# DRAM layout of the chain's operands in a hybrid decoder layer: five loads per half segment in place of ten

## The chip, the cores and the metric

The kernel runs on one core of a Trainium2 chip. The metric is the device time of one execution in microseconds (us), taken as the median of several runs. The engines are named as in the profile: PE (TensorE matmuls), PEld (its weight loads), DVE (VectorE), ACT (ScalarE), POOL (GpSimd), and SP (SyncE), whose queue issues all of the program's DMA transfers.

## The reference, cut to what matters

One layer over 2048 tokens of width 1024: a norm and an input projection, then two groups of eight heads of 64, RWKV-7 time mixing and a forgetting attention (FoX), a SiLU gate over both, the output projection and a final norm. The parts that matter here:

```python
def step(state, inp):                      # RWKV-7, per head: state is 64 x 64, 2048 steps
    rt, wt, kt, vt, kkt, at = inp
    sa = jnp.einsum('bhvk,bhk->bhv', state, -kkt)
    state = (state * wt[:, :, None, :] + sa[..., :, None] * (kkt * at)[..., None, :]
             + vt[..., :, None] * kt[..., None, :])
    yt = jnp.einsum('bhvk,bhk->bhv', state, rt)
    return state, yt
...
c = jnp.cumsum(log_f, axis=1)              # FoX: decay of each head along the sequence
s = jnp.einsum('bhqd,bhkd->bhqk', q, k) * scale + c[..., :, None] - c[:, :, None, :]
prob = softmax(where(causal, s, -inf)); o = prob @ v
```

## The kernel before, in words

The 2048 steps of RWKV-7 are cut into 32 chunks of 64 tokens. Heads go in pairs `p` (0 to 3); a pair fills the 128 partitions, head `h` of the pair in partitions 0 to 63 or 64 to 127 (`HR`).

First comes a preparation stage: for each pair and each block of 512 tokens, `prep` makes the operands of the chunks and stores them to DRAM. For half a block (four chunks) these are `d_ga` (lines 526 to 530), `d_gl` (line 550), `d_ar` (line 551), `d_nk` (line 562), and for a whole block `d_vn` (line 572). `inverse` adds `d_z`. FoX projections and gate projections are put between these pieces.

Then comes the chain: `chain` (line 724) runs the 32 chunks in order, because each needs the state of the one before. Its operands come back in half segments of two chunks: `half_seg` (line 703) loads a tile `G` from `d_ga` and `d_gl`, a tile `SV` from `d_vn`, `NK` and `AR`. `G` holds, for each pair and head, 64 partitions that come from `d_ga` and the other 64 that come from `d_gl`; `SV` holds values in one half of the partitions and the running state, which the chain writes itself, in the other. Each of the four tiles has three buffers, and a half segment is asked for four chunks ahead.

The attention of the FoX heads fills PE around the chain. `decay_setup` (line 873) prepares the decay of two heads and stores its two fp16 halves to `d_nc` (line 918); `head_max` (line 930) loads queries and keys of a head, and two rows of `d_nc` into `km` (line 939), and multiplies them (`sq`, line 952) to find row maxima; `head_loads` and `head_out` do the attention proper (`st`, `pv`).

The order of the instructions on each engine is not that of the text: the program is built with a planner that simulates a timeline (`schedule_with_timeline_sim=True`) and fixes each engine's queue by it. On the chip each queue then runs strictly in that order, SP's DMA queue included.

Of the kernel before, what the change touches and what calls it, by code (L numbers as in the profile page):

```python
# [20 lines left out]
S = 2048  # L21
# [18 lines left out]
def hymba_body(tc, x, norm_g, w_in, rw_mu, rw_w_up, rw_w0, rw_a_up, rw_a0, rw_k_k, rw_k_a, rw_r_k,  # L40
# [7 lines left out]
    with ctx:  # L48
# [3 lines left out]
        def dram(name, shape, dt=F32):  # L52
            return dr.tile(shape, dt, name=name)

        d_ga = dram("d_ga", [512, 32, 128])
        d_gl = dram("d_gl", [4, 128, 32, 128])
        d_ar = dram("d_ar", [4, 128, 32, 64])
        d_nk = dram("d_nk", [4, 128, 32, 128])
        d_vn = dram("d_vn", [4, 128, 32, 64])
        d_z = dram("d_z", [4, 128, 32, 64])  # L60
        d_bo = dram("d_bo", [512, S])
        d_q = [dram(f"d_q{i}", [512, S], F16) for i in range(2)]
# [2 lines left out]
        d_l = dram("d_l", [NB, 128, 2, TB])  # L65
        d_yr = dram("d_yr", [512, S])
        d_gate = dram("d_gate", [1024, S])
        d_nc = [dram(f"d_nc{i}", [8, S], F16) for i in range(2)]
        d_gs = dram("d_gs", [4, S], F16)
        d_yf = dram("d_yf", [S, 512])  # L70

# [339 lines left out]
        with c1:  # L411
# [59 lines left out]
            def prep(p, b, r, k, v, lw, mab):  # L471
# [48 lines left out]
                for hb in range(2):  # L520
                    h4 = slice(4 * hb, 4 * hb + 4)
                    hs = slice(8 * b + 4 * hb, 8 * b + 4 * hb + 4)
                    v_ = f"{u}_{hb}"
                    bk = T("bk" + v_, "bk", 2, (128, 4, 128))

                    ga = T("ga" + v_, "ga", 2, (128, 4, 128))
                    nc.vector.scalar_tensor_tensor(ga[:, :, 0:64], c3(nk)[:, h4], -1.0, c3(nlw)[:, h4],
                                                   ALU.mult, ALU.mult)
                    nc.gpsimd.tensor_tensor(ga[:, :, 64:128], c3(r)[:, h4], c3(nL)[:, h4], ALU.mult)
                    nc.sync.dma_start(d_ga[pc, hs, :], ga)  # L530

                    nc.vector.scalar_tensor_tensor(bk[:, :, 0:64], c3(th)[:, h4], 0.5, c3(eI)[:, h4], ALU.mult, ALU.mult)
                    nc.gpsimd.tensor_tensor(bk[:, :, 64:128], c3(k)[:, h4], c3(eI)[:, h4], ALU.mult)

                    gl = T("gl" + v_, "o2", 2, (128, 4, 128))
                    ar = T("ar" + v_, "ar", 1, (128, 4, 64))
                    pb = ps_r.tile([128, 4, 128], F32, name=f"pb{v_}", tag="r")
                    pk = ps_r.tile([128, 4, 128], F32, name=f"pk{v_}", tag="r")
                    for c in range(4):
                        for h, (q0, q1) in enumerate(HR):  # L540
                            nc.tensor.matmul(pb[q0:q1, c], bk[q0:q1, c, 0:64], ga[q0:q1, c], start=True, stop=True)
                        for h, (q0, q1) in enumerate(HR):
                            o0, o1 = HR[1 - h]
                            nc.tensor.matmul(pk[o0:o1, c], bk[q0:q1, c, 64:128], ga[q0:q1, c], start=True, stop=True)
                    nc.vector.tensor_tensor(mab[:, :, hs].rearrange("q t c -> q c t"), pb[:, :, 0:64],
                                            mk[:, 0:64].unsqueeze(1).to_broadcast([128, 4, 64]), ALU.mult)
                    nc.vector.tensor_tensor(ar, pb[:, :, 64:128],
                                            mk[:, 64:128].unsqueeze(1).to_broadcast([128, 4, 64]), ALU.mult)
                    nc.vector.tensor_tensor(gl, pk, mk.unsqueeze(1).to_broadcast([128, 4, 128]), ALU.mult)
                    nc.sync.dma_start(d_gl[p, :, hs, :], gl)  # L550
                    nc.sync.dma_start(d_ar[p, :, hs, :], ar)

                    nc.gpsimd.tensor_tensor(bk, bk, gam[:, p, hs].unsqueeze(2).to_broadcast([128, 4, 128]), ALU.mult)
                    nkt = T("nkt" + v_, "o2", 2, (128, 4, 128))
                    pn = ps_r.tile([128, 4, 128], F32, name=f"pn{v_}", tag="r")
                    for c in range(4):
                        nc.tensor.transpose(pn[:, c, :], bk[:, c, :], ident)
                    nc.scalar.activation(nkt[:, :, 0:64], pn[:, :, 0:64], AF.Copy)
                    for h, (q0, q1) in enumerate(HR):
                        o0, o1 = HR[1 - h]  # L560
                        nc.scalar.activation(nkt[o0:o1, :, 64:128], pn[q0:q1, :, 64:128], AF.Copy)
                    nc.sync.dma_start(d_nk[p, :, hs, :], nkt)
# [5 lines left out]
                for h in range(2):  # L568
                    o0, o1 = HR[1 - h]
                    for par, (q0, q1) in enumerate(HR):  # L570
                        nc.scalar.activation(vn[o0:o1, :, par, :], pv[q0:q1, :, h * 64:h * 64 + 64], AF.Copy)
                nc.sync.dma_start(d_vn[p, :, c8, :], vn.rearrange("q c e d -> q (c e) d"))

            def inverse(p, mab):

# [127 lines left out]
        def half_seg(hs):  # L703

            c2_ = slice(2 * hs, 2 * hs + 2)
            g_ = rp.tile([128, 4, 2, 2, 128], F32, name=f"G{hs}", tag="G", bufs=3)
            nk_ = rp.tile([128, 4, 2, 2, 64], F32, name=f"NK{hs}", tag="NK", bufs=3)
            ar_ = rp.tile([128, 4, 2, 64], F32, name=f"AR{hs}", tag="AR", bufs=3)
            sv_ = rp.tile([128, 2, 4, 2, 64], F32, name=f"SV{hs}", tag="SV", bufs=3)
            ga_v = d_ga.rearrange("(p q) c x -> q p c x", q=128)  # L710
            gl_v = d_gl.rearrange("p q c x -> q p c x")
            vn_v = d_vn.rearrange("p q c x -> q c p x")
            for h, (q0, q1) in enumerate(HR):
                o0, o1 = HR[1 - h]
                nc.sync.dma_start(g_[q0:q1, :, h], ga_v[q0:q1, :, c2_])
                nc.sync.dma_start(g_[o0:o1, :, h], gl_v[o0:o1, :, c2_])
                for c in range(2):
                    nc.sync.dma_start(sv_[o0:o1, c, :, h, :], vn_v[o0:o1, 2 * hs + c])
            nc.sync.dma_start(nk_.rearrange("q p c h d -> q p c (h d)"),
                              d_nk.rearrange("p q c x -> q p c x")[:, :, c2_])  # L720
            nc.sync.dma_start(ar_, d_ar.rearrange("p q c x -> q p c x")[:, :, c2_])
            return g_, nk_, ar_, sv_
# [107 lines left out]
        with c2:  # L830
# [42 lines left out]
            def decay_setup(p):  # L873
# [37 lines left out]
                nc.tensor.transpose(p3, f(w_), ident)  # L911
                nct = A(f"nct{p}", "nct", (32, 128))
                ts(nct, p3, -1.0 / GS, ALU.mult)
                nch = [A(f"nch{p}_{i}", f"nch{i}", (32, 128), F16) for i in range(2)]
                nc.vector.tensor_copy(nch[0], nct)
                nc.vector.tensor_tensor(nch[1], nct, nch[0], ALU.subtract)
                for i in range(2):
                    nc.sync.dma_start(d_nc[i][hs].rearrange("h (j q) -> (h j) q", q=128), nch[i])

            def v_setup(h):  # L920

# [8 lines left out]
            def head_max(h):  # L930
# [4 lines left out]
                nc.sync.dma_start(qb[0:64], d_q[0][r])  # L935
                nc.sync.dma_start(qb[64:66], d_gs[2:4])
                nc.sync.dma_start(km[0:64], d_k[0][r])
                for i in range(2):
                    nc.sync.dma_start(km[64 + i:65 + i], d_nc[i][h:h + 1])
                mx = ap_.tile([128, 16, 4], F32, name=f"mx{h}", tag="mx", bufs=2)  # L940
                nc.gpsimd.memset(mx, -3e38)
                for i in range(16):
# [213 lines left out]
```

## Time and profile before

| | |
|---|---|
| median of 3 runs | 1705.23 us (1697.16 to 1711.42) |
| the profiled execution | 1702.15 us, of which its span is 1700.4 us |
| PE, DVE, ACT, POOL busy | 92%, 67%, 52%, 45% of the span |
| mean granted TensorE clock | 0.963 |
| bytes moved | 207.71 MB, 122 GB/s in the mean |
| packets under 512 B, under 2 KB | 53664, 173472 of 211979 |

All parts below are read from the one profiled execution; the span runs from its first to its last instruction. A busy PE is a PE with a matmul in its pipeline, at whichever clock was granted. The idle time of an engine that does not set the end costs nothing.

### The profile page before, as it was taken

What the parts mean: (1) busy time and instruction counts of PE and PEld (TensorE: products, weight loads), DVE (VectorE), ACT (ScalarE), POOL (GpSimd) and SP (SyncE); (2) the same over time, 40 slices, a digit from 0 to 9 for tenths busy, and PEclk for the clock granted to TensorE, in tenths of its full rate; (3) what the DMA queues carried; (4) which work ended last, traced back from release to release, by engine and by line L of the source; (5) the groups of instructions that cost most, each with busy time, mean ns of one, the idle gap of its engine ahead of it and who ended that gap; (6) DMA issues with size and microseconds to landing.
All of it is one profiled execution on the core that took longest, in us unless ns stands there. A gap on an engine that the chain in (4) does not pass through costs nothing. (4 is left out here: it accounts for less than half of the span.)

```text
span 1700.4 us, 36186 instructions
## 1 busy us (share of the span) xinstructions
PE 1571.5 (92%) x14182; PEld 970.9 (57%) x14182; DVE 1137.3 (67%) x2442; ACT 889.1 (52%) x1683; POOL 756.8 (45%) x846
## 2 busy tenths in 40 slices
PE   4899799899999999899999999799999998899998
PEld 2455355455554564445454566566666665577886
DVE  5876468975797758843654578488898674754443
ACT  5634444444424454445334238487787868776221
POOL 5654554555335543532201126366666755753000
PEclk9799899999999999999999999799999998999999
DMA  6432232233213242322326019858688632733452
GB/s 181 124 100 87 96 109 90 83 121 116 98 68 119 78 149 85 118 84 85 117 84 157 32 45 226 194 137 199 158 198 193 163 85 67 227 100 101 156 172 87
DMA packets 211979, 207.71 MB, mean 122 GB/s; under 512 B 53664, under 2 KB 173472, under 8 KB 211296
## 3 DMA queue, kind: packets, MB, share of 16 engines
q1 hardware_dynamic: 211808, 205.39, 42.1%
q8 instruction: 112, 1.84, 0.5%
q14 instruction: 59, 0.48, 0.1%
HBM read 123.34 MB, written 81.94 MB: 121 GB/s over the span
## 5 line engine op out<-in xcount | busy, mean ns | idle before, releaser
L1010 POOL TENSOR_TENSOR pl<-p,ph 128x512 f16<-128x512 f32 (+3 forms) x216 | 233.2, 1088 | 172.7 <-ACT p L1008 135.2
L1007 ACT ACTIVATE ph<-st,be 128x512 f16<-128x512 f32 (+1 forms) x320 | 202.4, 633 | 95.0 <-PE st L1003 40.3
L956 DVE TENSOR_REDUCE mx<-sq 128x1 f32<-128x384 f32 (+6 forms) x320 | 184.7, 603 | 50.8 <-PE sq L955 31.4
L1008 ACT ACTIVATE p<-st,be 128x512 f32<-128x512 f32 (+1 forms) x320 | 202.7, 634 | 5.5 <-POOL pl L1010 3.4
L332 PE MATMUL pf<-fh_f,hhi 128*128 128x386 f16 x512 | 169.5, 332 | 2.1 <-DVE fl L348 2.1
L332 PE MATMUL pf<-fl_f,hhi 128*128 128x386 f16 x512 | 168.2, 328 | 1.2 <-POOL fl_f L219 1.2
L332 PE MATMUL pf<-fh_f,hlo 128*128 128x386 f16 x512 | 168.5, 329 | 0.0
L254 PE MATMUL pj_r<-hhi,wh_r 128*128 128x512 f16 x384 | 148.9, 388 | 0.0
L254 PE MATMUL pj_r<-hlo,wh_r 128*128 128x512 f16 x384 | 148.7, 387 | 0.0
L254 PE MATMUL pj_r<-hhi,wl_r 128*128 128x512 f16 x384 | 148.5, 387 | 0.0
L341 POOL TENSOR_TENSOR fr<-ft,nhalf 128x4 f32<-128x4 f32 x64 | 65.3, 1021 | 175.1 <-DVE ft L101 169.0
L332 PEld LDWEIGHTS <-hhi 128*128 128x128 f16 x1024 | 99.3, 99 | 75.6 <-issue 12.0
L1018 PE MATMUL pv<-va,pl 128*128 128x65 f16 x1088 | 131.4, 196 | 7.7 <-POOL pl L1010 4.3
L1014 PE MATMUL pv<-va,ph 128*128 128x65 f16 x1088 | 131.8, 196 | 2.6 <-DVE ot L1023 1.7
L1016 PE MATMUL pv<-vb,ph 128*128 128x64 f16 x1088 | 131.7, 194 | 0.0
L952 PE MATMUL sq<-km,qb 66*128 66x384 f16 (+6 forms) x320 | 107.9, 357 | 21.6 <-DMA km<-d_nc 14.7
L254 PEld LDWEIGHTS <-wh_r 128*128 128x128 f16 x768 | 75.6, 100 | 87.3 <-issue 9.2
L1018 PEld LDWEIGHTS <-pl 128*128 128x128 f16 x1088 | 101.5, 98 | 32.8 <-POOL pl L1010 11.5
L999 PE MATMUL st<-qa,ka 128*128 128x512 f16 (+1 forms) x320 | 113.9, 358 | 5.4 <-ACT p L1008 3.5
L1000 PE MATMUL st<-qb,kb 68*128 68x512 f16 (+1 forms) x320 | 113.8, 358 | 0.8 <-DMA kb<-d_gs 0.8
L1014 PEld LDWEIGHTS <-ph 128*128 128x128 f16 x1088 | 102.0, 99 | 17.6 <-DVE ot L1023 2.6
L1010 DVE TENSOR_TENSOR pl<-p,ph 128x512 f16<-128x512 f32 (+3 forms) x104 | 77.2, 742 | 44.4 <-ACT p L1008 31.5
(376 smaller groups left out, 4005.2 us busy)
## 6 DMA issues: line engine op xcount, KB each, us to landing
d_ga<-ga SPq DMA_DIRECT2D x32, 256.0 KB
d_gl<-gl SPq DMA_DIRECT2D x32, 256.0 KB
d_nk<-nkt SPq DMA_DIRECT2D x32, 256.0 KB
d_gate<-gv SPq DMA_DIRECT2D x32, 256.0 KB
G<-d_ga SPq DMA_DIRECT2D x32, 256.0 KB
G<-d_gl SPq DMA_DIRECT2D x32, 256.0 KB
NK<-d_nk SPq DMA_DIRECT2D x16, 512.0 KB
xr<-in_x_dram SPq DMA_DIRECT2D x16, 512.0 KB
```

The costliest lines, as they stand in the source:

```text
L254: nc.tensor.matmul(ps, a[:, kt, o:o + 128], h[:, kt, :], start=n == 0, stop=n == 3 * KT - 1)
L332: nc.tensor.matmul(ps, a[:, kt, js], w[:, kt, :], start=n == 0, stop=n == 3 * KT - 1)
L952: nc.tensor.matmul(ps[:, :w], qb[0:66, i * 128:i * 128 + 128], km[0:66, ks], start=True, stop=not last)
L956: nc.vector.tensor_reduce(mx[:, i, b:b + 1], ps[:, :w], AX.X, ALU.max)
L999: nc.tensor.matmul(ps[:, c0:], ka[:, k0:k0 + 128], qa[:, q0 + c0:q0 + 512], start=True, stop=False)
L1000: nc.tensor.matmul(ps[:, c0:], kb[0:68, k0:k0 + 128], qb[0:68, q0 + c0:q0 + 512], start=False, stop=not diag)
L1007: nc.scalar.activation(ph[:, c0:], ps[:, c0:], AF.Exp, bias=be[:, h, qb_, j:j + 1])
L1008: nc.scalar.activation(p32[:, c0:], ps[:, c0:], AF.Exp, bias=be[:, h, qb_, j:j + 1])
L1010: eng.tensor_tensor(pl[:, c0:], p32[:, c0:], ph[:, c0:], ALU.subtract)
L1014: nc.tensor.matmul(pv[:, qq, 0:65], ph[:, s_], vh[:, j, 0:65], start=j == 0 and qq == 0, stop=False, skip_group_check=True)
L1016: nc.tensor.matmul(pv[:, qq, 0:64], ph[:, s_], vl[:, j], start=False, stop=False, skip_group_check=True)
L1018: nc.tensor.matmul(pv[:, qq, 0:65], pl[:, s_], vh[:, j, 0:65], start=False, stop=fin, skip_group_check=True)
```

## The change

`d_ga` and `d_gl` become one tensor `d_g`, laid out by pair and head, in the order in which the tile `G` holds its 128 partitions; `prep` stores each of the two operands in two halves of 64 partitions. One load of 128 partitions (1 MB) then fills `G` where there were four of 64 partitions (256 KB each). `d_vn` is laid out by partition and chunk, so that two loads fill `SV` where there were four; its store now writes runs of 256 B (64 values of one chunk and pair) in place of 2 KB. The two halves of the decay become one tensor `d_nc`, stored one head at a time, and one load of two partitions brings both rows of a head to `km` where there were two. All values, matmuls and bytes moved stay as they are.

```diff
-        d_ga = dram("d_ga", [512, 32, 128])
-        d_gl = dram("d_gl", [4, 128, 32, 128])
+        d_g = dram("d_g", [4, 2, 128, 32, 128])
-        d_vn = dram("d_vn", [4, 128, 32, 64])
+        d_vn = dram("d_vn", [128, 32, 4, 64])
-        d_nc = [dram(f"d_nc{i}", [8, S], F16) for i in range(2)]
+        d_nc = dram("d_nc", [8, 2, S], F16)
...                                                       in prep
-                    nc.sync.dma_start(d_ga[pc, hs, :], ga)
+                    for h, (q0, q1) in enumerate(HR):
+                        nc.sync.dma_start(d_g[p, h, q0:q1, hs, :], ga[q0:q1])
-                    nc.sync.dma_start(d_gl[p, :, hs, :], gl)
+                    for h, (q0, q1) in enumerate(HR):
+                        o0, o1 = HR[1 - h]
+                        nc.sync.dma_start(d_g[p, h, o0:o1, hs, :], gl[o0:o1])
-                nc.sync.dma_start(d_vn[p, :, c8, :], vn.rearrange("q c e d -> q (c e) d"))
+                nc.sync.dma_start(d_vn[:, c8, p, :], vn.rearrange("q c e d -> q (c e) d"))
...                                                       in half_seg
-            for h, (q0, q1) in enumerate(HR):
+            nc.sync.dma_start(g_.rearrange("q p h c x -> q (p h) (c x)"),
+                              d_g.rearrange("p h q c x -> q (p h) c x")[:, :, c2_].rearrange("q a c x -> q a (c x)"))
+            for h in range(2):
                 o0, o1 = HR[1 - h]
-                nc.sync.dma_start(g_[q0:q1, :, h], ga_v[q0:q1, :, c2_])
-                nc.sync.dma_start(g_[o0:o1, :, h], gl_v[o0:o1, :, c2_])
-                for c in range(2):
-                    nc.sync.dma_start(sv_[o0:o1, c, :, h, :], vn_v[o0:o1, 2 * hs + c])
+                nc.sync.dma_start(sv_[o0:o1, :, :, h, :].rearrange("q c p d -> q (c p) d"),
+                                  d_vn[o0:o1, c2_].rearrange("q c p d -> q (c p) d"))
...                                                       in decay_setup
-                for i in range(2):
-                    nc.sync.dma_start(d_nc[i][hs].rearrange("h (j q) -> (h j) q", q=128), nch[i])
+                nch = A(f"nch{p}", "nch", (32, 2, 128), F16)
+                nc.vector.tensor_copy(nch[:, 0], nct)
+                nc.vector.tensor_tensor(nch[:, 1], nct, nch[:, 0], ALU.subtract)
+                for h in range(2):
+                    nc.sync.dma_start(d_nc[2 * p + h].rearrange("i (j q) -> j i q", q=128), nch[16 * h:16 * h + 16])
...                                                       in head_max
-                for i in range(2):
-                    nc.sync.dma_start(km[64 + i:65 + i], d_nc[i][h:h + 1])
+                nc.sync.dma_start(km[64:66], d_nc[h])
```

## Rows read from the trace of the kernel before

**Rows 1.** The page, part 1, its line of engines.
```profile
PE 1571.5 (92%) x14182; PEld 970.9 (57%) x14182; DVE 1137.3 (67%) x2442; ACT 889.1 (52%) x1683; POOL 756.8 (45%) x846
```

**Rows 2.** Stretches: start:end, length, busy us and count by engine, PE clock, DMA share, GB/s.
```profile
core 0: us, PE busy (x) PEld busy (x) DVE busy (x) ACT busy (x) POOL busy (x), PEclk, DMA share, GB/s
1036.00:1071.30 35.30, 34.05 (x577) 23.65 (x576) 27.86 (x64) 27.13 (x53) 20.15 (x21) 1.00 1.06 244
1071.30:1080.90 9.60, 0.06 (x2) 0.13 (x2) 0.00 (x0) 0.00 (x0) 1.11 (x3) 0.62 0.73 132
1080.90:1097.40 16.50, 16.50 (x143) 10.77 (x143) 7.50 (x18) 6.75 (x14) 4.60 (x6) 0.50 0.83 187
1097.40:1418.00 320.60, 307.46 (x4915) 213.18 (x4915) 257.46 (x540) 251.82 (x481) 202.74 (x207) 0.99 0.67 157
```

**Rows 3.** Waits of PE over the whole span: total, times, longest (us).
```profile
PE sq L952 <- DMA km<-d_nc: 14.7, 3, 9.5
...
PE sq L952 <- DMA qb<-d_q: 2.9, 2, 1.6
```

**Rows 4.** The chain that ended last, 1060 to 1083 us: start, length, what.
```profile
1062.28 0.52 SPq L715
...
1065.01 9.94 DMA G<-d_gl
1075.01 4.01 DMA d_nc<-nch
...
1079.36 1.47 DMA km<-d_nc
```

**Rows 5.** Timeline of SP's queue, 1062.8 to 1081.3 us: start, length, issue.
```profile
1065.01 0.66 SPq L716 DMA_DIRECT2D G<-d_gl  x1
...
1069.51 0.53 SPq L719 DMA_DIRECT2D NK<-d_nk  x1
1070.33 3.56 SPq L718 DMA_DIRECT2D SV<-d_vn  x3
1075.01 1.25 SPq L918 DMA_DIRECT2D d_nc<-nch  x2
```

**Rows 6.** Timeline of SP's queue, 1111 to 1120 us.
```profile
1111.57 0.36 SPq L1025 DMA_DIRECT2D d_yf<-ot  x1
1112.07 0.59 SPq L715 DMA_DIRECT2D G<-d_ga  x1
...
1114.01 0.61 SPq L716 DMA_DIRECT2D G<-d_gl  x1
1119.24 0.36 SPq L719 DMA_DIRECT2D NK<-d_nk  x1
```

**Rows 7.** Three stretches in which one kind of transfer filled the DMA queue.
```profile
1112.00:1113.50 1.50, 1.50 (x21) 0.89 (x20) 1.50 (x5) 0.97 (x3) 0.00 (x0) 1.00 0.45 90
1115.00:1118.00 3.00, 3.00 (x59) 2.20 (x56) 3.00 (x6) 2.95 (x7) 3.00 (x3) 1.00 1.13 206
1121.00:1122.00 1.00, 1.00 (x24) 0.76 (x21) 0.97 (x2) 0.88 (x3) 0.85 (x3) 1.00 1.04 358
```

**Rows 8.** Timeline of SP's queue, 1199 to 1204 us.
```profile
1199.69 0.92 SPq L918 DMA_DIRECT2D d_nc<-nch  x2
1202.32 1.53 SPq L939 DMA_DIRECT2D km<-d_nc  x4
```

**Rows 9.** Two stretches around an idle PE, and one after a short wait.
```profile
718.85:722.20 3.35, 0.00 (x1) 0.02 (x1) 3.35 (x7) 0.54 (x1) 2.08 (x4) 0.97 0.55 205
722.20:728.80 6.60, 6.59 (x40) 3.16 (x41) 4.32 (x9) 0.88 (x3) 2.81 (x5) 0.50 0.17 62
1204.60:1210.00 5.40, 5.40 (x91) 3.96 (x92) 5.11 (x10) 4.07 (x7) 2.31 (x2) 1.00 0.25 63
```

**Rows 10.** Waits of SP's queue over the span, and the issues that write d_ga.
```profile
SPq L530 <- DVE ga L527: 72.5, 25, 7.3
...
L530 SPq DMA_DIRECT2D d_ga<-ga x32: 319/320/383, 94.3 to 793.5; - x32
```

More of the change, by code (lines that the diff above doesn't have):

```diff
@@ L709, in half_seg @@
             sv_ = rp.tile([128, 2, 4, 2, 64], F32, name=f"SV{hs}", tag="SV", bufs=3)
-            ga_v = d_ga.rearrange("(p q) c x -> q p c x", q=128)
-            gl_v = d_gl.rearrange("p q c x -> q p c x")
-            vn_v = d_vn.rearrange("p q c x -> q c p x")
-            for h, (q0, q1) in enumerate(HR):
+            nc.sync.dma_start(g_.rearrange("q p h c x -> q (p h) (c x)"),
+                              d_g.rearrange("p h q c x -> q (p h) c x")[:, :, c2_].rearrange("q a c x -> q a (c x)"))
+            for h in range(2):
                 o0, o1 = HR[1 - h]
-                nc.sync.dma_start(g_[q0:q1, :, h], ga_v[q0:q1, :, c2_])
-                nc.sync.dma_start(g_[o0:o1, :, h], gl_v[o0:o1, :, c2_])
-                for c in range(2):
-                    nc.sync.dma_start(sv_[o0:o1, c, :, h, :], vn_v[o0:o1, 2 * hs + c])
+                nc.sync.dma_start(sv_[o0:o1, :, :, h, :].rearrange("q c p d -> q (c p) d"),
+                                  d_vn[o0:o1, c2_].rearrange("q c p d -> q (c p) d"))
             nc.sync.dma_start(nk_.rearrange("q p c h d -> q p c (h d)"),
@@ L913, in decay_setup @@
                 ts(nct, p3, -1.0 / GS, ALU.mult)
-                nch = [A(f"nch{p}_{i}", f"nch{i}", (32, 128), F16) for i in range(2)]
-                nc.vector.tensor_copy(nch[0], nct)
-                nc.vector.tensor_tensor(nch[1], nct, nch[0], ALU.subtract)
-                for i in range(2):
-                    nc.sync.dma_start(d_nc[i][hs].rearrange("h (j q) -> (h j) q", q=128), nch[i])
+                nch = A(f"nch{p}", "nch", (32, 2, 128), F16)
[3 more added lines that the diff above has]
+                    nc.sync.dma_start(d_nc[2 * p + h].rearrange("i (j q) -> j i q", q=128), nch[16 * h:16 * h + 16])
             def v_setup(h):
```

## The prediction, made before the change was run

> **What bounds the kernel now.** I read the page first, then the stretches, then PE's waits, and last the chain that ended last. PE is busy for 1571.5 of 1700.4 us [rows 1], far above any other engine: matmuls set the time, and an edit on transfers can give back only what PE loses by waiting and by a lowered clock. The idle time is about 129 us, and transfers of this change's kind stand behind one large piece of it. In the chain's stage PE does 0.06 us of work between 1071.3 and 1080.9 us, and the stretch after it, 16.5 us long, runs at a granted clock of 0.50 (the 1.2 GHz level) where the stretches beside it have 0.99 to 1.00 [rows 2]. The waits name the cause: `sq` waits for `km<-d_nc`, 14.7 us in three waits, the longest 9.5 [rows 3]. Nothing in PE's waits names `G`, `SV`, `NK` or `AR`: the chain's own loads come in time.
>
> The chain of waits tells why `km` was late [rows 4]. The decay had been computed and the issue of its store to `d_nc` came at 1075.01, after 9.94 us in which SP's queue hung on the landing of a `G` load issued at 1065.01; the store took 4.01 us to be seen, the load of `km` 1.47. The store has nothing to do with that `G` load. Between the two, SP's timeline shows seven issues: `km<-d_k`, two to `qb`, `NK`, three to `SV` [rows 5]. So the store is the eighth transfer after it, and I read this as a queue that lets about eight transfers be under way: each issue first waits for the landing of the eighth before it. The three `SV` issues, 3.56 us for three where one alone takes about 0.6, are held in the same way [rows 5]. This is the place where fewer and larger transfers can count.
>
> The cost of this stall now: 9.5 us of idle time, and 16.5 us at half clock, in which PE does what it could do in 8.25. Together 17.8 us.
>
> **The change part by part. The load of G.** Four issues of 256 KB become one of 1 MB. Where `G` loads alone fill the queue (issues at 1112.07 to 1114.01, 64 partitions each [rows 6]) the rate is 206 GB/s at a full DMA share; where an `NK` load of 128 partitions is alone (issue at 1119.24, held a while by its buffer [rows 6]) it is 358 GB/s [rows 7]. Both move runs of 1 KB, so what differs is the partitions. I therefore let the new load run at 358: 1.05 MB take 2.9 us for 5.1, 2.2 us less in each of 16 half segments, 35 us of transfer time in all. Nearly all of that is hidden beside the chain. What counts is the load just ahead of the `d_nc` store, and it enters below as a shorter time for that store; the bound on the other side is 206 GB/s as now, with the store as slow as now.
>
> Two pages of the Trainium skill differ here. "DMA: Bandwidth & Descriptors", Rules for kernel authors, says that transfers to two partition halves serialize because each half already uses all 16 engines, by which the rate of a half would be that of the whole. "SBUF — State Buffer", Door 1: The DMA port swizzle, says that bandwidth follows the number of ports that the partitions reach, half of them for 64 partitions. The trace's 206 against 358 sides with the second; by the first alone the store would stay at its 4.0 us below and the stall would be 1.4 us longer.
>
> **Issues in the chain's stage.** Each half segment loses five issues of some 0.6 us, 16 times 3 us; SP is no bound there, so this is hidden beside the chain. What counts is the place in the count of eight: the store of `d_nc` then has `G`, `km<-d_k`, two to `qb`, `NK` and one or two `SV` ahead of it, six or fewer, and its eighth predecessor is older than the `G` load. So it isn't held by landings. It still stands behind `NK`, which went out at 1069.51 [rows 5], waiting for the chain to free its buffer, and behind two `SV` issues: 1069.5 + 0.6 + 2 x 0.6 = 1071.3 us, 3.7 earlier than now. From the issue of this store to that of the load that reads it, the quieter case of another pair of heads takes 1202.32 - 1199.69 = 2.6 us [rows 8], against 4.0 here; I take 2.6, as the faster `G` has drained by then, and keep 4.0 for the range. Then 1.5 us for the load and 0.3 for its issue: `sq` starts at 1075.7 in place of 1080.9. The idle time falls from 9.5 to 4.4 us.
>
> **The clock.** After an idle stretch of 3.35 us in the preparation the clock was 0.50 for 6.6 us; after the wait of about 2.3 us that ended at 1204.6 it stayed at 1.00 [rows 9]. With 4.4 us the first is nearer: 6.6 us at half clock, 3.3 us lost, against 8.25 now. The stall costs 4.4 + 3.3 = 7.7 us in place of 17.8: **10.1 us gained**. The bounds are 0 (the order or the queue keeps it as it is) and 17.8 (the planner puts the store ahead of `NK`, where it could go out at 1065.01 + 0.66, about 1066, and land in time).
>
> **The load of km.** One load for two rows of a head. The other two waits of `sq` on it sum to 14.7 - 9.5 = 5.2 us [rows 3]. They go through the same store and one issue less: four `km` issues take 1.53 us [rows 8], two would take half. I count 0.4 us each, **0.8 us**; the bounds are 0 and 5.2, and 2.9 more for the waits on `qb<-d_q` [rows 3], which stand in the same queue.
>
> **The stores.** Each of 32 `d_ga` and 32 `d_gl` stores becomes two: 64 issues more of 0.32 us, 20.5 us of SP over the preparation [rows 10]. SP waits 72.5 us for `ga` at these very issues [rows 10]: it arrives early, so this is covered, and I count 0. Behind it stand the weight loads and `lw`; if the cover were gone the price would be 0.64 us in each of 32 half blocks, 20.5 us at most. The 16 `d_vn` stores now write runs of 256 B. The nearest row is the `d_yf` store of 128 KB in such runs (issue at 1111.57 [rows 6]), at 90 GB/s with a DMA share of 0.45 [rows 7]: 0.26 MB then take 2.9 us each. `SV` is read only in the chain's stage, when the preparation has ended, so nobody waits: 0. Even if all were paid, 16 x 2.9 = 46 us of transfers lie in a stage in which PE does not name `d_vn`. The same DMA page, Specifications, states that runs under 512 B lose line rate to read-modify-write; it bears on these stores alone.
>
> **The order.** The planner lays every queue anew when the transfers change. The trace of before can't show the result; its nearest price is one more or one fewer stall such as the one above, 17.8 us either way. I take 0.
>
> **The sum.** 1702.15 - 10.1 - 0.8 = 1691.3 us against the profiled execution, which lies 3.1 us below the median of the runs. Against the median: 1705.2 - 10.9 = **1694 us**, 0.6% faster. The three runs of before spread by 14 us, so a change of about 1% is what a measurement of this kernel can tell from none.
>
> **The rivals.** *The stall goes wholly.* The store is placed early enough, the clock stays up, and the small waits shrink too: 1705.2 - 17.8 - 5 = 1682 us. For it: the chain names a landing as what releases the store, not the engine that makes the decay [rows 4], so the decay was ready by 1065, and the planner sees fewer issues on SP. Against: in SP's order `NK` and its buffer wait come first, and PE's order puts `sq` where the planner believes the data to be. *Nothing moves.* The bytes are the same, and `sq` needs a store and a load that run one after the other through the same queue; if the planner moves `sq` forward by what SP gains, the wait is as long: 1705 us. For it: the DMA share is 1.06 from 1036 to 1071 [rows 2], full whatever the count of transfers. *A longer queue in front of the small transfers, slower.* Eight places now hold at most 512 KB each (`NK`); with loads of 1 MB they hold more bytes, and a small store or `km` row issued behind them waits for all of them. It decides when SP's order puts a 1 MB load between `d_nc` and `km` of a later pair, where now the waits are 2 us: then one more stall of the same size, 1705.2 + 17.8 = 1723 us. Against: in a queue served in order the bytes ahead of a given transfer are the same.
>
> **How the numbers follow.** The forecast has 0.42 (1688 to 1703), the stall gone 0.23, nothing 0.20, slower 0.15. The range leaves out the slower case and the far end of the stall gone: 1677 to 1714, the upper end being "nothing" plus half of the spread of the runs, with rounding. Faster by over 1% means under 1688: the second case and about a fourth of the first, 0.34; slower by over 1% is 0.15; the rest is 0.51.
>
> **What would show it.** In the changed kernel's profile: `G` loads at some 350 GB/s where they are alone; the `d_nc` store issued within 2 us of `NK` and not released by a `G` landing; PE's wait for `km<-d_nc` at 4 to 5 us, with a short stretch at 0.50 behind it; no wait of PE on `G` or `SV`; the preparation as long as before. The prediction is wrong if a wait of 9 us or more stands in the chain's stage again, under whatever name, or if the preparation's length moves by more than some 10 us, which would be the planner's order and not the transfers.

## The result, and the profile after

The changed kernel takes 1687.65 us (median of six runs) where the kernel before takes 1706.95 beside it: a ratio of 0.9891, with a 95% interval of 0.9859 to 0.9923. It is about 1.1% faster. One of the six runs, 1780.67 us at a mean granted clock of 0.844, was a slow one, and the ratio leaves it out. The profiled execution takes 1691.52 us, of which its span is 1689.8.

The page's line of engines answers to [rows 1]. PE's busy time is 2.4 us less, the span 10.6 us: the same matmuls, with less idle time and a higher clock (0.969 in the mean, 0.963 before).

```profile
PE 1569.1 (93%) x14182; PEld 968.4 (57%) x14182; DVE 1135.4 (67%) x2442; ACT 890.4 (53%) x1683; POOL 756.3 (45%) x846
```

To find where the 10.6 us lie, I cut both spans at the same instructions: the last `pj_r` (the preparation of the chain ends), the last `pf` (the FoX projections end), the last `pY` (the chain ends). The stretches of before, columns as in [rows 2]:

```profile
773.20:1020.40 247.20, 240.80 (x1793) 130.14 (x1792) 140.29 (x365) 93.77 (x166) 49.08 (x57) 0.99 0.27 86
1020.40:1418.00 397.60, 372.03 (x5817) 256.65 (x5816) 308.24 (x655) 299.95 (x575) 238.69 (x246) 0.96 0.72 168
1418.00:1700.40 282.40, 261.82 (x1984) 198.17 (x1982) 137.66 (x210) 141.69 (x286) 95.30 (x86) 0.97 0.42 134
```

and of the changed kernel:

```profile
772.50:1024.90 252.40, 243.95 (x1793) 131.18 (x1792) 139.78 (x365) 94.07 (x167) 49.31 (x57) 0.98 0.28 85
1024.90:1404.20 379.30, 366.28 (x5814) 253.66 (x5813) 308.07 (x655) 299.72 (x575) 238.88 (x246) 0.99 0.68 176
1404.20:1689.80 285.60, 262.60 (x1985) 198.22 (x1984) 136.05 (x210) 142.35 (x286) 94.01 (x86) 0.96 0.41 133
```

The chain's stretch falls from 397.6 to 379.3 us, 18.3 less, and its clock rises from 0.96 to 0.99. The stretch ahead of it grows by 5.2 us and the one behind by 3.2; the preparation ends at 772.5 in place of 773.2. PE's waits, which answer to [rows 3]:

```profile
PE sq L950 <- DMA km<-d_nc: 4.6, 2, 4.2
...
PE sq L950 <- DMA qb<-d_gs: 1.7, 2, 1.3
```

and SP's own waits from 1055 to 1078 us:

```profile
SPq L937 <- DMA d_nc<-nch: 3.8, 1, 3.8
...
SPq L917 <- DMA G<-d_g: 0.7, 1, 0.7
```

Of the 4.6 us for `km`, 4.2 are the wait for the first pair of heads, ahead of the chain's stage. At the second pair, where 9.5 us were lost, 0.4 is left. The stretch up to the first `sq` there, the one behind it (at a clock of 1.00, where [rows 2] had 0.50), and the new `G` load alone:

```profile
1068.90:1076.00 7.10, 5.90 (x125) 4.65 (x122) 4.57 (x11) 4.93 (x12) 4.17 (x5) 1.00 0.66 112
1076.00:1092.00 16.00, 15.80 (x240) 11.13 (x240) 11.30 (x27) 11.04 (x22) 8.44 (x11) 1.00 1.01 275
1104.00:1105.00 1.00, 1.00 (x18) 0.68 (x17) 1.00 (x3) 1.00 (x3) 1.00 (x2) 1.00 1.04 359
```

The new load runs at 359 GB/s, against 206 for the four of before [rows 7]. SP's timeline at this place answers to [rows 5]:

```profile
1058.65 1.33 SPq L712 DMA_DIRECT2D G<-d_g  x1
1060.08 3.44 SPq L936 DMA_DIRECT2D km<-d_k  x1
1063.60 0.58 SPq L978 DMA_DIRECT2D qb<-gh  x1
1064.28 0.54 SPq L979 DMA_DIRECT2D qb<-gl  x1
1064.91 0.54 SPq L718 DMA_DIRECT2D NK<-d_nk  x1
1065.56 2.32 SPq L716 DMA_DIRECT2D SV<-d_vn  x2
1067.92 0.62 SPq L720 DMA_DIRECT2D AR<-d_ar  x1
1069.33 1.37 SPq L917 DMA_DIRECT2D d_nc<-nch  x2
1074.53 0.57 SPq L937 DMA_DIRECT2D km<-d_nc  x2
```

The `d_nc` store is the eighth transfer behind the `G` load, as it was before: there is one `SV` issue less between them, but `AR` moved ahead. And SP's wait names the landing of that `G` load as what let the store go. So the store is held by the same rule; it only goes out earlier.

Where the eight comes from stands in the two traces: each transfer of SP tells its landing by a semaphore, and there are eight of them, used in strict turn (810 of the 818 transfers of before have the semaphore of the eighth before them). The store shares one with the `G` load and goes out 0.06 us after its last update, at 1075.01 after 1074.95 us before and at 1069.33 after 1069.27 here. The count is thus that of the program's semaphores. How many transfers the queue itself would hold is shown by no run.

How much earlier the store goes out has to be counted from PE's place in the program, because PE came here later than before (the stretch ahead grew). The matmul `cumT`, PE's last step in the decay's computation for this pair, is such a mark; it starts at 1060.3 us in the trace of before and at 1064.8 here. PE was free for `sq` 11.0 us after it before, where it began to wait at 1071.3 [rows 2], and 10.8 here (1076.0 less the wait of 0.4). The last instruction that makes the decay's halves ends 3.3 us after the mark in both. The store went out 14.7 us after the mark before, and 4.5 here: that is where the stall went. Which part of the 10.2 us is the `G` load's own, and which was there before, is counted below, beside the run that brings the stall back.

### The profile page after: what moved, and what is told of

Same layout as the page of the kernel before. It is cut to its first block, busy times and chain, and to the rows that moved or that the text cites. A ratio compares the mean times of both kernels' runs of the same rounds, so it can differ in the third digit from the quotient of the medians.

```text
span 1689.8 us, 36160 instructions
## 1 busy us (share of the span) xinstructions
PE 1569.1 (93%) x14182; PEld 968.4 (57%) x14182; DVE 1135.4 (67%) x2442; ACT 890.4 (53%) x1683; POOL 756.3 (45%) x846
## 5 line engine op out<-in xcount | busy, mean ns | idle before, releaser
L1016 PEld LDWEIGHTS <-pl 128*128 128x128 f16 x1088 | 101.3, 98 | 36.8 <-DVE pl L1008 10.4
L950 PE MATMUL sq<-km,qb 66*128 66x384 f16 (+6 forms) x320 | 106.8, 354 | 10.3 <-DMA km<-d_nc 4.6
```

Of the source, the lines that this page charges most:

```text
L1016: nc.tensor.matmul(pv[:, qq, 0:65], pl[:, s_], vh[:, j, 0:65], start=False, stop=fin, skip_group_check=True)
```

## The experiments

The theory to be tested is the width: what shortens the stall is the rate of the `G` loads, by their 128 partitions, since SP's issues wait for landings. A load of 128 partitions is called wide here, one of 64 narrow. The rivals are the count (fewer transfers in the queue of eight) and the order (the planner laid the queues anew). The first four were run on one chip beside the kernel before, the next four and the last four likewise; ratios are to the kernel before that was run beside them.

**G alone.** The new layout and single load of `G`, with the rest as before.

```diff
...                                                       layout and stores of d_g as in the change
+            nc.sync.dma_start(g_.rearrange("q p h c x -> q (p h) (c x)"), d_g...[:, :, c2_]...)
             for h in range(2):
-                nc.sync.dma_start(g_[q0:q1, :, h], ga_v[q0:q1, :, c2_])
-                nc.sync.dma_start(g_[o0:o1, :, h], gl_v[o0:o1, :, c2_])
```

> The kernel before with the G part of the change alone: d_g laid out by head, stores in halves, one load of 128 partitions and 1 MB; SV and d_nc as before. Queue theory (the d_nc store was held by the landings of the eighth transfer before it, and fewer transfers ahead free it): three issues fewer ahead of the store, it goes out some 5 us earlier after the cumulative sum than before (14.6 us there), PE's longest wait for km falls from 9.5 to 0 to 3 us, time 1688 to 1694. Rate theory (64-partition loads run at 206 GB/s, 128-partition loads at 350): the same sign, 1690 to 1697. Rival, order (the planner's new queue order is what helped, not the transfers): the stall may stay or not, time anywhere within 10 us of 1706.

Measured: 1696.61 us, 0.9965 (0.9939 to 0.999). The stall at the second pair shrinks to 1.6 us, but the third and fourth pairs now wait 3.5 and 4.3:

```profile
PE sq L952 <- DMA km<-d_nc: 12.9, 4, 4.3
```

**G by four wide loads.** The same layout, one load of 128 partitions for each pair: the old number of transfers at the new width.

```diff
+            for p in range(4):
+                nc.sync.dma_start(g_[:, p]..., d_g[p]...[:, :, c2_]...)
```

> As the G part alone, but G is loaded by four transfers of 256 KB, one for each pair, of 128 partitions each: as many issues as before, wider. This parts the two theories. Rate theory: G loads at some 350 GB/s, the landings ahead of the d_nc store come 2 us sooner for each half segment in the queue, the wait for km falls to 3 to 6 us, time 1692 to 1699. Queue theory alone: as many transfers as before, the store is held as before, wait 8 to 10 us, time 1702 to 1710.

Measured: 1705.2 us, 1.0016 (0.9996 to 1.0037). The stall at the second pair is 2.1 us, so four wide loads shorten it nearly as one does; but the time is that of before, and at the fourth pair a wait of 7.9 us appears. SP's timeline there shows how: the two stores of the decay's halves are parted by four held `SV` issues, 4.50 us for four.

```profile
1292.88 0.32 SPq L919 DMA_DIRECT2D d_nc<-nch  x1
1293.30 0.38 SPq L720 DMA_DIRECT2D NK<-d_nk  x1
1293.86 4.50 SPq L719 DMA_DIRECT2D SV<-d_vn  x4
1299.79 0.38 SPq L722 DMA_DIRECT2D AR<-d_ar  x1
1300.27 0.45 SPq L919 DMA_DIRECT2D d_nc<-nch  x1
...
1301.65 0.24 SPq L940 DMA_DIRECT2D km<-d_nc  x1
```

So the time is the one expected of the count, but the stall is not: it falls even below what was expected of the rate, and the other waits take the gain away.

**G by two narrow loads.** The new layout, loaded in two halves of 64 partitions: fewer transfers at the old width.

```diff
+            for q0, q1 in HR:
+                nc.sync.dma_start(g_[q0:q1]..., d_g...[q0:q1, :, c2_]...)
```

> As the G part alone, but G is loaded by two transfers of 512 KB, each of 64 partitions: half the issues of before, the old width. Rate theory alone: 206 GB/s as before, the wait for km stays at 8 to 10 us, time 1702 to 1710. Queue theory: two issues fewer ahead of the store, it is held by a transfer two places earlier, the wait falls to 3 to 7 us, time 1692 to 1700.

Measured: 1713.03 us, 1.0057 (1.0036 to 1.0079); 8.7 us at the second pair. Two narrow loads in place of four gain nothing; the kernel is 0.6% slower.

**SV alone.** The layout of `d_vn` and the two `SV` loads.

```diff
-        d_vn = dram("d_vn", [4, 128, 32, 64])
+        d_vn = dram("d_vn", [128, 32, 4, 64])
...                                                       store of d_vn as in the change
-                for c in range(2):
-                    nc.sync.dma_start(sv_[o0:o1, c, :, h, :], vn_v[o0:o1, 2 * hs + c])
+                nc.sync.dma_start(sv_[o0:o1, :, :, h, :]..., d_vn[o0:o1, c2_]...)
```

> The kernel before with the SV part of the change alone: d_vn by partition and chunk, its store in runs of 256 B, two loads for four; G as before. Queue theory: two issues of 1.3 us that were held by landings go from in front of the d_nc store, which goes out 2 to 3 us sooner; wait for km 6 to 8 us, time 1699 to 1706. Rate theory: no change, the SV loads stay at 64 partitions. If the 256 B runs of the store cost anything it is in the preparation: its end (last pj_r matmul at 773 us before) moves by more than 3 us; expected 0.

Measured: 1705.66 us, 1.0013 (0.9991 to 1.0035). The preparation ends no later (last `pj_r` at 769.0 us; 768.0 with the decay rows alone, which leave it as it is), so the stores in runs of 256 B cost nothing there. The waits on `km` move to the later pairs, 19.4 us in four. At the second pair the wait is 3.8 us, but not because the store is early: it goes out 12.4 us after `cumT`, and PE, in another order, is free for `sq` only 16.2 us after it, where it was 11.0 before.

**The decay rows alone.** One tensor `d_nc`, stored per head, one load for both rows.

```diff
...                                                       layout and stores of d_nc as in the change
-                for i in range(2):
-                    nc.sync.dma_start(km[64 + i:65 + i], d_nc[i][h:h + 1])
+                nc.sync.dma_start(km[64:66], d_nc[h])
```

> The kernel before with the d_nc part of the change alone: one store and one load of km for a head where there were two halves each; G and SV as before. Of the runs so far, the G part alone gave 0.9965, the SV part 1.0013, so the sum of the parts misses the whole (0.989) by some 10 us. Theory 1, the round trip d_nc to km is what PE waits for and this part shortens it for all pairs: waits for km from 14.7 us to under 8, time 1692 to 1698. Theory 2, the part does nothing by itself (0.3 us an issue), the whole is more than its parts because it needs a short queue ahead of the store as well: time 1702 to 1710 with the wait of 8 to 10 us where it was.

Measured: 1715.09 us, 1.0053 (1.003 to 1.0076), with 11.0 us at the second pair. The order of PE's instructions here is that of "G by two narrow loads" in all but 14 of 14182 places, and the ratio is the same: four narrow loads or two, under one order. That speaks against the count, though the two differ in the decay rows as well. The time lies above both ranges that were expected.

**The change without the decay rows.** `G` and `SV` as changed, `d_nc` as before.

```diff
...                                                       layout and stores of d_nc as before
-                nc.sync.dma_start(km[64:66], d_nc[h])
+                for i in range(2):
+                    nc.sync.dma_start(km[64 + i:65 + i], d_nc[i][h:h + 1])
```

> The change without its d_nc part. If the queue ahead of the store (G and SV) is what counts: 1686 to 1693, as the whole change, the waits for km under 5 us. If the d_nc part or the order that the planner makes with it is needed: 1697 to 1705, with waits of 3 to 5 us at the later pairs as in the run with the G part alone.

Measured: 1695.12 us, 0.9948 (0.9926 to 0.9971). No wait on `km` at the second and third pairs, 3.3 us at the fourth. The decay rows, which alone make the kernel slower, are worth some 0.5% as the last part of the whole (0.9948 here, 0.9891 and 0.9911 with them). That fourth wait goes with them; but PE's order changes in 4871 places too, so what the rest comes from is not shown.

**The decay early, in both kernels.** The decays of pairs 0 to 2 are computed at once ahead of the attention, so that their stores lie well before their loads.

```diff
-                        if h % 2 == 0:
-                            decay_setup((h + 2) // 2)
+                        if h == -2:
+                            for p in range(3):
+                                decay_setup(p)
+                        elif h == 4:
+                            decay_setup(3)
```

> The kernel before with its layouts and transfers as they are; the decays of pairs 0 to 2 are prepared one after the other ahead of the attention, pair 3 as before. This takes the round trip d_nc to km out of the chain's stage for pairs 1 and 2 without touching a chain load. If the waits for km are what the chain's loads cost PE: no wait of 9 us in the chain's stage, 17.8 us for the stall and some 2 for the second wait gone, time 1682 to 1690. Rival, the waits only show a limit that lies elsewhere (the chain's own latency, the DMA bytes): another wait takes their place and the time is 1698 to 1708.

> The changed kernel with the same early decays. If nothing but the round trip to km was gained by the change, it has little left to win here and ends within 5 us of the early decays with the old transfers, both at 1680 to 1688. If wider and fewer loads are worth something of their own (shorter stretches of a full DMA queue, qb and ka loads sooner), it is 5 to 12 us faster than those: 1672 to 1682.

Measured: 1727.72 us in the kernel before, 1.0147 (1.0116 to 1.0177), and 1721.33 in the changed one, 1.0099 (1.007 to 1.0127). No wait of PE names `km` any more; others, of up to 5.7 us, stand in its place, here in the kernel before:

```profile
PE sq L952 <- DMA qb<-d_q: 6.3, 2, 4.6
PE pU L749 <- DMA zc<-d_z: 5.7, 1, 5.7
PE sq L952 <- DMA qa<-d_q: 4.5, 1, 4.5
```

Both are slower than any of the ranges expected. Taking the wait away in this way is thus no gain. Why the whole becomes 1.5% slower than before is not settled: the planner laid every queue anew. The change is still worth 6.4 us between these two, without any wait on `km`.

**The changed kernel again, and its G by two narrow loads.** The first is the changed kernel, unedited, to measure the other against. The second loads `G` in two halves and leaves all else as changed.

```diff
-            nc.sync.dma_start(g_.rearrange("q p h c x -> q (p h) (c x)"), d_g...)
+            for q0, q1 in HR:
+                nc.sync.dma_start(g_[q0:q1]..., d_g...[q0:q1, :, c2_]...)
```

> The changed kernel once more, unchanged, beside the three below on one chip: ratio to the kernel before 0.986 to 0.993 (1684 to 1694 us), PE's waits for km in the chain's stage under 2 us. It tells how much of the distance between the whole and its parts is noise.

> The changed kernel with G loaded by two transfers of 64 partitions (512 KB each) in place of one of 128; layouts, stores, SV and d_nc as in the change. One issue more for each half segment, and the old width. If the width of the load is what pays: G loads back at 206 GB/s, 2.2 us later for each half segment, and the wait for km returns at the second pair with 5 to 9 us; 1698 to 1710 us. If the number of transfers is what pays: within 4 us of the changed kernel.

Measured: 1687.9 us, 0.9911 (0.9884 to 0.9937), and 1706.66 us, 1.0035 (1.0011 to 1.0059). The two run the same order on DVE, ACT and POOL, and on PE in all but 18 of 14182 places; SP's queue has the second `G` issue and takes some other issues ahead of this place in another order, though from this `G` load to the store the order is the same. So under one order of the compute engines the width of `G`, with what SP's queue makes of it, is worth 18.8 us, no less than the whole gain beside it (16.2). In the repeat, the chain's stretch:

```profile
1021.00:1396.00 375.00, 361.76 (x5813) 250.78 (x5812) 307.88 (x655) 299.20 (x575) 238.90 (x246) 1.00 0.69 178
```

and PE's only wait for `km` in it, at the second pair:

```profile
PE sq L950 <- DMA km<-d_nc: 1.0, 1, 1.0
```

With the narrow loads the stall is back. The stretch in which PE does nothing, the one behind it at half clock, and a stretch in which `G` alone is loaded:

```profile
1074.50:1081.00 6.50, 0.00 (x0) 0.00 (x0) 0.00 (x0) 0.00 (x0) 1.10 (x3) 0.76 0.56 96
1081.00:1108.50 27.50, 27.43 (x235) 17.65 (x235) 12.27 (x27) 11.64 (x23) 8.12 (x9) 0.50 0.81 184
1121.00:1123.00 2.00, 2.00 (x38) 1.44 (x35) 2.00 (x5) 1.95 (x5) 2.00 (x2) 1.00 1.15 208
```

It costs 6.5 us of idle time, and 27.5 us at 0.50 in which 13.7 are lost: 20.3 us. It is the stall of [rows 2], 3.1 us shorter in idle time and 11 longer at the low clock. This execution takes 1717.27 us, 10.6 above its kernel's median, so the 27.5 us need not be usual; what the stall costs in the median run is not shown. SP's queue there:

```profile
1062.45 2.81 SPq L713 DMA_DIRECT2D G<-d_g  x2
...
1068.20 0.53 SPq L720 DMA_DIRECT2D NK<-d_nk  x1
...
1074.44 2.72 SPq L919 DMA_DIRECT2D d_nc<-nch  x2
1079.45 0.58 SPq L939 DMA_DIRECT2D km<-d_nc  x2
```

and SP's wait ahead of the store:

```profile
SPq L919 <- DMA G<-d_g: 1.5, 1, 1.5
```

The store again goes out when a `G` load has landed, the eighth transfer before it. Counted from `cumT`, with the issues of `G` from each SP timeline:

| us after `cumT` | before | two narrow loads | changed kernel | repeat |
|---|---|---|---|---|
| `cumT` starts at | 1060.3 | 1063.5 | 1064.8 | 1061.1 |
| first `G` load of the chain's stage | -40.1 | -40.1 | -40.1 | -40.1 |
| first issue of the fourth `G` load | 0.6 | -1.1 | -6.2 | -5.7 |
| store of `d_nc` issued | 14.7 | 10.9 | 4.5 | 5.6 |
| load of `km` issued | 18.7 | 15.9 | 9.7 | 10.3 |
| first `sq` | 20.6 | 17.5 | 11.2 | 11.8 |
| idle PE before it | 9.5 | 6.6 | 0.4 | 1.0 |

The first `G` load of the stage goes out as the last `pf` runs, in all four 40.1 us ahead of `cumT`; so SP starts level. Between the narrow loads and the changed kernel the store moves by 6.4 us. Of these, 5.1 are there already when SP comes to the fourth `G` load, the one that holds the store; only 1.3 come between it and the store. There SP, early as it is in the changed kernel, waits for PE ahead of `km<-d_k`, longer than with the narrow loads (second line):

```profile
SPq L936 <- PE st L998: 3.2, 1, 3.2
SPq L938 <- PE pv L1018: 1.0, 1, 1.0
```

From the store on, the steps are alike. So what the width gives is above all SP's lead over the compute engines, built up by the loads ahead. From the first `G` load to the fourth SP moves the same data in all kernels of the table below, with the DMA engines full (a share of 0.94 to 1.07); the stretch in the kernel before, and in the changed one:

```profile
1020.23:1060.96 40.73, 39.10 (x580) 25.87 (x578) 35.59 (x79) 33.88 (x65) 23.89 (x26) 1.00 1.00 220
1024.72:1058.65 33.93, 32.30 (x470) 21.02 (x469) 29.84 (x61) 28.55 (x55) 19.71 (x20) 1.00 1.03 267
```

**The small transfers from another queue.** The stores to `d_nc` and the loads of `km` from it are issued by GpSimd, in the kernel before and in the changed one.

```diff
-                    nc.sync.dma_start(d_nc[i][hs]..., nch[i])
+                    nc.gpsimd.dma_start(d_nc[i][hs]..., nch[i])
...
-                    nc.sync.dma_start(km[64 + i:65 + i], d_nc[i][h:h + 1])
+                    nc.gpsimd.dma_start(km[64 + i:65 + i], d_nc[i][h:h + 1])
```

> The kernel before, but the d_nc stores and the km loads from d_nc are issued from GpSimd's queue, which has a ring and landing counts of its own; every chain load as before. If the stall of 9.5 us comes of the place of these two in SP's queue: the wait for km falls under 3 us at every pair, time 1682 to 1692. If another transfer of the same head (qb, km from d_k) then ends last, or GpSimd's waits hold up its subtractions for the attention: 1698 to 1712.

> The changed kernel with the same two transfers on GpSimd's queue. If the change gained only by the round trip to km, this is no faster than the changed kernel by more than the waits left there, 4 us: 1680 to 1690. If GpSimd's in-order wait costs more than it frees: 1690 to 1705.

Measured: 1709.79 us, 1.0039 (1.002 to 1.0059), and 1708.58 us, 1.0023 (1.0005 to 1.004). The stall at the second pair is gone from the kernel before, but its issue now stands in POOL's queue, which waits 7.2 us for the first part of `km`, and PE waits for what POOL makes. POOL's waits from 1060 to 1090 us:

```profile
POOL km L939 <- DMA km<-d_k: 7.2, 1, 7.2
```

and PE's over the span:

```profile
PE pv L1018 <- POOL pl L1010: 9.4, 10, 4.6
...
PE sq L952 <- DMA km<-d_nc: 3.8, 1, 3.8
```

The changed kernel loses its whole gain in this way, and between these two kernels the change is worth 1.2 us. None of the versions beats the changed kernel.

**The kernels with the decays in place and all transfers on SP's queue, in one view.** The time that SP takes from the first `G` load of the chain's stage to the fourth; the issue of the load of `km`, after `cumT`, at the second pair; the waits of `sq` for `km` at the four pairs of heads; and the DMA share from 1020 to 1400 us, in which every one of these kernels moves 172 to 175 GB/s:

| kernel | G load | first to fourth `G` (us) | `km` load after `cumT` (us) | waits for `km`, pairs 1 to 4 (us) | DMA share | ratio |
|---|---|---|---|---|---|---|
| before | 4 narrow | 40.7 | 18.7 | 2.8, 9.5, 2.3, 0 | 0.75 | 1 |
| the decay rows alone | 4 narrow | 43.1 | 20.2 | 4.4, 11.0, 2.6, 3.6 | 0.73 | 1.0053 |
| SV alone | 4 narrow | 40.0 | 18.3 | 3.0, 3.8, 4.9, 7.8 | 0.77 | 1.0013 |
| G by two narrow loads | 2 narrow | 41.1 | 17.7 | 2.9, 8.7, 3.5, 5.5 | 0.76 | 1.0057 |
| changed, two narrow loads | 2 narrow | 39.0 | 15.9 | 4.2, 6.6, 0.3, 0 | 0.78 | 1.0035 |
| G by four wide loads | 4 wide | 36.4 | 10.6 | 3.0, 2.1, 2.5, 7.9 | 0.65 | 1.0016 |
| G alone | 1 wide | 35.1 | 10.2 | 3.5, 1.6, 3.5, 4.3 | 0.64 | 0.9965 |
| changed, without the decay rows | 1 wide | 34.2 | 10.4 | 3.4, 0, 0, 3.3 | 0.66 | 0.9948 |
| the changed kernel | 1 wide | 33.9 | 9.7 | 4.2, 0.4, 0, 0 | 0.68 | 0.9891 |
| the changed kernel again | 1 wide | 34.4 | 10.3 | 4.4, 1.0, 0, 0 | 0.68 | 0.9911 |

The stretch from which the DMA share is read, in the kernel before:

```profile
1020.00:1400.00 380.00, 355.43 (x5523) 244.88 (x5521) 295.57 (x630) 285.81 (x549) 229.69 (x238) 0.96 0.75 174
```

and in the changed one:

```profile
1020.00:1400.00 380.00, 366.98 (x5774) 253.62 (x5773) 310.40 (x662) 299.28 (x574) 238.90 (x248) 0.99 0.68 175
```

The DMA share falls by about 0.1 with the width of the `G` load and not with the number of loads. SP's time to the fourth `G` load and the issue of the `km` load part wide from narrow without overlap, whatever the order: 33.9 to 36.4 us against 39.0 to 43.1, and 9.7 to 10.6 against 15.9 to 20.2. The number of transfers counts for little beside it: one wide load for four takes 1.3 us off the time to the fourth `G`, two `SV` loads for four 0.7 and 0.9, two narrow `G` loads for four nothing or 1.0. For SP's lead, and with it the stall at the second pair, the width is shown as the cause; for the time it is shown by the two kernels of one order. It is not enough by itself: four wide loads alone give 1.0016. The order counts beside it: the waits at the third and fourth pairs differ from kernel to kernel without regard to the width, so the parts don't add up to the whole.

## Why the prediction was right, and where it was not

The time, 1687.65 us, lies in the range and 6 us below the forecast, and the change is faster as forecast. That the sum came so near is in part luck, as the last points show: the stall gave back more than its term, and the order took some of it away. Point by point:

*The bound and the stall: right.* PE is the bound, and what the change gives back is the stall at `km<-d_nc` with its low clock. Put at 17.8 us, it costs 20.3 in the one execution that brings it back, and the chain's stretch is 18.3 us shorter without it.

*The rate of G: right.* 359 GB/s when alone, 208 in the two narrow halves of the changed layout. Both move runs of 1 KB, and both under the same order; the partitions make the difference. On the two pages of the Trainium skill that the prediction weighed: two halves do run one after the other, as "DMA: Bandwidth & Descriptors", Rules for kernel authors, says, but each at the lower rate that "SBUF — State Buffer", Door 1: The DMA port swizzle, gives for half of the ports. The trace agrees with both: two halves under way together move at 208 GB/s, one whole load at 359. By the first page's rule alone the width would pay nothing, and the two kernels differ by 18.8 us.

*Where the rate enters: the step that failed.* The prediction wrote of the 35 us of transfer time, "Nearly all of that is hidden beside the chain. What counts is the load just ahead of the `d_nc` store", and took 2.2 us for it. But SP's queue issues strictly in order and its issues wait for landings, and from the first `G` load of the stage to the fourth the DMA engines are full (a share of 1.00 before); so what each earlier `G` load saves brings all later issues forward. Three loads at 2.2 us make 6.6; when SP comes to the fourth it is 5.1 us further on than with narrow loads, and 1.3 come behind it. The term that the prediction hid is the larger one.

*The count of eight: the wait was right, the count wrong.* The store was put at "six or fewer" transfers behind `G` and so not held. The planner put `AR` ahead of it, it is again the eighth, and SP's wait names the `G` landing. The eight, read as the queue's, is the number of the program's semaphores. And fewer transfers bring SP forward by 1.3 us at most in the pairs above, where the width brings 4.4 to 6.1 (four narrow loads against four wide, two against one).

*NK as the new hold: wrong.* The prediction took 1069.51 us, the issue of `NK`, as set by the chain's buffer. In the changed kernel `NK` goes out at 1064.91, 0.63 us after the issue before it. In the trace of before it had followed just as closely, 0.65 us behind the second issue to `qb`; it was this one that had waited, for the landing of the eighth transfer before it:

```profile
SPq L981 <- DMA gg<-d_gate: 1.5, 1, 1.5
```

*From the store to the load: mis-sized.* 2.6 us was taken, with a bound of 4.0; it is 5.2 (1069.33 to 1074.53), and 5.0 with the narrow loads. The forecast that `sq` starts at 1075.7 us came true to 0.3 us (1076.0) by luck: the issue is 2.0 us earlier than forecast, and what follows it is 2.3 longer.

*The idle time and the clock: mis-sized.* Forecast 4.4 us of idle time and 3.3 lost to the clock; measured 0.4 and none. PE's place in the order was taken from the trace of before, 1071.3 us, but PE came there 4.3 us later, at 1075.6. The rival "the stall goes wholly" describes the chain's stage. It is not that PE was only late: in the repeat, where `cumT` starts at 1061.1 us, 0.8 later than before, the wait is 1.0 us, and the clock of the whole chain's stretch 1.00. The rival with the longer queue does not show: at the third and fourth pairs `sq` waits for no `km`.

*The load of km: the size right, by luck.* The two other waits were to fall by 0.8 us and fall by 0.9 (4.2 for 5.1); but the one at the first pair grows by 1.4, and the one at the third goes.

*The stores: right.* The preparation is as long as before (772.5 and 773.2 us), with 64 issues more and `d_vn` in short runs.

*The order: taken as 0, and it is not.* Of the 18.3 us won in the chain's stage, 8.4 go elsewhere. Ahead of the chain the first `km` wait is 4.2 us for 2.8 and `ka` 1.7 for 0.4, and the low clock behind is longer. The stretch around them in the kernel before:

```profile
900.00:930.00 30.00, 26.18 (x121) 11.53 (x120) 15.96 (x45) 11.41 (x16) 6.81 (x3) 0.94 0.61 158
```

and in the changed kernel:

```profile
900.00:930.00 30.00, 24.08 (x104) 10.48 (x103) 14.85 (x47) 10.93 (x14) 6.51 (x3) 0.89 0.66 164
```

That is 2.1 us less work and, with 0.11 and 0.06 of 30 us, some 1.5 us of clock: 3.6 of the 5.2. In the kernel before SP issues this pair's store 3.9 us after its `cumT` (907.55 after 903.7), between `va` and `vb`; in the changed kernel 5.3 us after it (911.34 after 906.0), behind both. `sq` then comes 12.3 and 13.8 us after `cumT`. That this one place in SP's order is the cause was argued from the two timelines, not tried. Behind the chain, where the change has no transfer, PE's waits in the changed kernel (first line) are headed by one that is short in the trace of before (second line):

```profile
PE pv L1016 <- DVE pl L1008: 5.0, 7, 1.4
PE pv L1018 <- DVE pl L1010: 0.8, 2, 0.5
```

It stands with 5.0 us in seven waits in the run with two narrow loads too, which has the same order, and with 4.3 in five in the repeat. It is enough for the 3.2 us, and the new order is what these three share; that it comes of the order was not tried.

*The sum: a term too small and one left out.* The two profiles lie 10.6 us apart, near the forecast of 10.9, but the medians 19.3: the profile of before is 4.8 us below its median, that of the changed kernel 3.9 above. The repeat, with a profiled execution of 1683.94 us, is 18.2 below that of before: 22.6 us less in the chain's stretch (375.0 for 397.6), 7.3 more around it, and 2.9 less in the preparation. Against this, 10.1 for the stall were too few, and the order's 0 was too good.

Open: why early decays cost 1.5% and what the change is worth 6.4 us by there, why the planner puts `sq` ahead of its data at the later pairs in the kernels with one part alone, and what would remove the first wait of 4.2 us.

## What to carry to other kernels

Load with all 128 partitions where a tile is filled by halves: where the DMA engines are full and the issues stand strictly in order, the time saved on each large load is not hidden, but brings every small dependent transfer behind it forward. Look which landing let a small store go, and by which semaphore, and count times from a mark on the engine that waits, not from the start of the span. In a program that a planner orders, test one part of a change by taking it out of the whole and checking that the engines' orders stayed; parts built alone get other orders, with waits of their own.

## What the runs showed of the hardware

After 6.5 us without work the clock stayed at 0.50 for 27.5 us, though PE was busy for 27.43 of them (16.5 us after 9.6 in [rows 2]). Loads in runs of 1 KB move at 206 to 208 GB/s into 64 partitions and at 358 to 359 into 128. With the DMA engines full, the small store to `d_nc` at the second pair takes 4.0 us in the kernel before, and 4.8 to 5.2 in the changed one and with its two narrow loads, from its issue to that of the load that reads it. The issue itself did not grow with the transfer: 0.43 us for `G` with its 1 MB where nothing holds it (at 1080.72), 0.54 for `NK` with half of that.
